# Reciprocal row sums applied after the weighted sum, and split keys and queries passed through DRAM, in the attention stage of a hybrid decoder kernel

## The chip, the cores and the metric

The kernel runs on one core of a Trainium2 chip. The metric is device time in microseconds (us) of one execution. The core has five engines that run their own instruction queues in order: TensorE (PE in the profile, with its weight loads listed apart as PEld), VectorE (DVE), ScalarE (ACT), GpSimd (POOL) and SyncE (SP), whose queue issues all DMAs of this kernel. PSUM is the memory that TensorE writes; SBUF is the on-chip memory that all engines read and write; DRAM tensors are reached by DMA only.

## What is computed

The reference is a two-layer decoder trunk over 1040 tokens (16 learned meta tokens and 1024 real ones) of width 1024. Layer 0 is a gated linear recurrence with a convolutional feed-forward block, layer 1 is the attention that the change is about, again with a feed-forward block. The attention (16 heads of width 64, a decay `c` per head and token, softmax over earlier tokens):

```
q = (x @ w_q).reshape(Bsz, T, B_HEADS, B_HDIM).transpose(0, 2, 1, 3)
...
for s, e in bounds:
    logits = jnp.einsum("bhqd,bhkd->bhqk", q[:, :, s:e], k[:, :, :e]).astype(jnp.float32) * scale
    logits = logits + (c[:, :, s:e, None] - c[:, :, None, :e])
    mask = jnp.arange(s, e)[:, None] >= jnp.arange(e)[None, :]
    p = jax.nn.softmax(jnp.where(mask, logits, -1e30), axis=-1)
    outs.append(jnp.einsum("bhqk,bhkd->bhqd", p.astype(v.dtype), v[:, :, :e]))
o = jnp.concatenate(outs, axis=2).transpose(0, 2, 1, 3).reshape(Bsz, T, D_MODEL)
return o @ w_out
```

## The kernel before, in words

Features lie on the 128 partitions and tokens along the free dimension. Each fp32 operand of a large matrix product is split into a high and a low part (`split`, lines 96 to 98: ACT casts a copy, DVE subtracts it from the source), and a product is three matmuls: high by high, high by low, low by high (lines 145, 148, 149). A matmul of 342 columns is the common size.

The attention stage weaves two streams into one hand-made order on TensorE (`weave`, in a manual schedule; the other engines' queues are ordered by the framework's scheduler). The first stream, `scores_ahead`, goes through 48 steps: 16 heads by three query blocks of 342 tokens (`BLK_B`), step s being head s // 3 and block s % 3. In step s it emits the weighted sums of step s (`sum_steps`) interleaved with the scores of step s + 1 (`score_steps`). The second stream, `dense`, projects values, keys and queries of the next pair of heads (`project`, in the order v0 v1 v2 k0 q0 k1 q1 k2 q2, the digit being the block), and at the end begins the output projection (`one`).

What one step does. `score_steps` takes three tiles of 114 queries. Per tile, TensorE multiplies the split queries by the split keys into PSUM (lines 879, 880) and adds the causal mask (line 882); DVE adds the decays and takes the row minimum (line 884, tile `L`); ACT takes the exponential with the row sum as a by-product (line 887, into `c4`); DVE takes the reciprocal of the sum (line 888) and multiplies the row tile by it (line 889). `sum_steps` turns the probabilities by TensorE transposes (line 909, PSUM tile `g`), ACT copies the high part out (line 913, `pTh`), DVE subtracts the low part (line 914, `pTl`), and two matmuls per key tile accumulate the output in the one `po` buffer of PSUM (lines 921, 922). The transposes run two key tiles ahead of the sums (`AHEAD`). At the end of a step ACT copies one half of `po` and DVE adds the other half (lines 933, 934), and SP writes 64 rows to the DRAM tensor `o_dram` (line 936).

Keys and queries. `project` leaves the scaled product of a pair of heads in one tile each (`k` in unit 17, `q` in unit 18; lines 798, 800). `halves(n, i)` then builds, for head n and block i, the operands of the score matmuls: `ks` with the high part of the keys on one half of the partitions and the low part on the other half (ACT line 837, DVE line 838), and two query tiles `qs` (high over low, and low over high; ACT lines 841, 842, 844, DVE line 843). That is four ACT and two DVE instructions of 64 partitions for each of 48 calls. Because the pair's tiles are reused, the dense stream waits before it writes k or q until the preceding pair's second head has been split. `halves` also loads the decays, broadcast from `c_dram` to 128 partitions (line 835). The first pair is projected earlier, by `heads0`, between the blocks of the preceding normalisation (`post`).

SP's queue in this stage holds the output writes of line 936, the decay loads of line 835 and the weight loads of line 115. GpSimd multiplies each loaded weight tile by the norm gain (line 126). Temporary tiles come from small rings: `u`, `y`, `sq` and `acc` have two buffers, `sq2` and `rstd` one (`SMB`).

Of the kernel before, what the change touches and what calls it, by code (L numbers as in the profile page):

```python
# [55 lines left out]
def tile_yoco(ctx: ExitStack, tc: tile.TileContext, hT, gains, lbl, w_in, head_g, w_oa,  # L56
# [228 lines left out]
    c_dram = nc.dram_tensor("csum", [BH, T], F32, kind="Internal").ap()  # L285

# [474 lines left out]

    KS, QS, VS, CN = [24, 25], [(33, 34), (6, 7)], [[35, 36], [4, 5]], [12, 13]
# [21 lines left out]
    def project(which, hp, i):  # L784

        p = pair[hp]
        if which not in p:
            src, c0, g, u = {"k": (kv_w, 0, 8, 17), "v": (kv_w, D, 8, 16), "q": (w_q, 0, 4, 18)}[which]
            p[which] = (WA.cols(src, [c0 + hp * P], gsb[:, g]), unit(u, which))
# [4 lines left out]
        while hp and which != "v" and ("split", 2 * hp - 1, i) not in seen:  # L794
            yield None
        with tc.high_priority(offset=OFF):
            if which == "q":
                V.scalar_tensor_tensor(dst[:, sl], pt, -HD ** -0.5, r2[:, sl], ALU.mult, ALU.mult)
            else:
                V.tensor_mul(dst[:, sl], pt, r2[:, sl])  # L800
# [25 lines left out]
    def halves(n, i):  # L826
# [6 lines left out]
        a, b = (hi, lo) if n % 2 else (lo, hi)  # L833
        sl = slice(BLK_A[i][0], BLK_A[i][0] + BLK_A[i][1])
        nc.sync.dma_start(h["c"][:, sl], c_dram[n:n + 1, sl].to_broadcast([P, BLK_A[i][1]]))
        x, k = pair[n // 2]["k"][1], h["k"]
        A.copy(k[a, sl], x[a, sl])
        V.tensor_sub(k[b, sl], x[a, sl], f(k[a, sl]))
        sl = slice(BLK_B[i][0], BLK_B[i][0] + BLK_B[i][1])
        x, (q1, q2) = pair[n // 2]["q"][1], h["q"]  # L840
        A.copy(q1[a, sl], x[a, sl])
        A.copy(q2[b, sl], x[a, sl])
        V.tensor_sub(q2[a, sl], x[a, sl], f(q1[a, sl]))
        A.copy(q1[b, sl], f(q2[a, sl]))
# [19 lines left out]
    def score_steps(s):  # L864
# [4 lines left out]
        out = h[g] = []  # L869
        for i in range(3):  # L870
# [5 lines left out]
            for x, (a, b) in enumerate(pcs):  # L876
# [9 lines left out]
                if last:  # L886
                    A.activation(L[:QT, :kn], L[:QT, :kn], AF.Exp, scale=-1.0, bias=c4[:, x:x + 1], accum_out=c4[:, 5:6])
                    V.reciprocal(c4[:, 6:7], c4[:, 5:6])
                    V.tensor_scalar(L[:QT, :kn], L[:QT, :kn], c4[:, 6:7], None, ALU.mult)  # L889
# [3 lines left out]
    def sum_steps(s):  # L893
# [31 lines left out]
        for kt in range(nk + AHEAD):  # L925
            if kt < nk:
                yield turned(kt)
            if kt >= AHEAD:
                yield summed(kt - AHEAD)
        r, r_ = (hi, lo) if j else (lo, hi)  # L930
        hp, sl = n // 2, slice(g0, g0 + gn)
        ot = o_last[0][:, sl] if hp == KT - 1 else tmp("sq", gn)
        A.copy(ot[r], av[r, :gn])
        V.tensor_add(ot[r], ot[r], av[r_, :gn])
        if hp < KT - 1:
            nc.sync.dma_start(o_dram[hp][r, sl], ot[r])
# [139 lines left out]
```

## Time and profile before

| what | value |
|---|---|
| median of 3 runs | 2878.49 us (2877.14 to 2882.29) |
| the profiled execution | 2883.05 us, its span 2881.1 us |
| PE, PEld busy | 2768.6 us (96%), 2709.2 us (94%) |
| DVE busy | 1830.8 us (64%) |
| ACT busy | 1258.2 us (44%) |
| POOL busy | 369.6 us (13%) |
| DMA | 163.14 MB, mean 57 GB/s |

Busy times are of the whole span. The page's slices of DVE go from 5 tenths in the feed-forward blocks to 8 tenths in the attention, so that an average over the span says little about this stage; the stage lies between about 1455 and 2040 us. PEclk in a window is the granted TensorE clock as a share of its upper level. Idle time of the weight loads (PEld) shows a wait of TensorE more sharply than that of PE, since matmuls are pipelined and their modelled durations overlap.

### The profile page before, as it was taken

Reading aid. Unit: us, or ns where it says so; the run is one execution under the profiler, and the core shown is the slowest. Engines: PE = TensorE matmul, PEld = TensorE weight load, DVE = VectorE, ACT = ScalarE, POOL = GpSimd, SP = SyncE. Lnnn points to the kernel's source line nnn. Section 1 sums busy time; section 2 is a strip of 40 time slices with the busy share of each in tenths; the row PEclk is TensorE's granted clock in tenths of the full one; section 3 lists DMA queues with packets and bytes.
Section 4 is the critical chain, followed back from the end, with each engine's and each line's share of the span. In section 5 each row is a group of like instructions: output and inputs, shape, how many; then the busy total and the mean of one; then the engine's idle time right before and its main releaser. Section 6 shows DMA issues by size and latency. Waiting matters only on the chain. (4 is left out here: it accounts for less than half of the span.)

```text
span 2881.1 us, 45581 instructions
## 1 busy us (share of the span) xinstructions
PE 2768.6 (96%) x17706; PEld 2709.2 (94%) x17706; DVE 1830.8 (64%) x3737; ACT 1258.2 (44%) x2421; POOL 369.6 (13%) x741
## 2 busy tenths in 40 slices
PE   8999999989999999999889999999989999999997
PEld 8999999989999999999789988898989999999997
DVE  5545445285655655566878888887684665565566
ACT  6445445455322322233566666666555232232232
POOL 2000000041100000004400000000240100010012
PEclk9999999999999999999899999999999999999999
DMA  4111111142211111112311111112242111121103
GB/s 132 30 38 30 38 40 49 37 125 62 66 38 52 45 52 38 44 52 67 92 45 45 45 45 45 45 45 93 70 124 59 45 52 52 30 65 39 52 30 113
DMA packets 202921, 163.14 MB, mean 57 GB/s; under 512 B 13984, under 2 KB 194128, under 8 KB 202704
## 3 DMA queue, kind: packets, MB, share of 16 engines
q1 hardware_dynamic: 202704, 160.23, 19.2%
q8 instruction: 138, 2.26, 0.3%
q14 instruction: 79, 0.65, 0.1%
HBM read 139.53 MB, written 20.66 MB: 56 GB/s over the span
## 5 line engine op out<-in xcount | busy, mean ns | idle before, releaser
L145 PE MATMUL pj<-x,wh 128*128 128x342 f32 (+1 forms) x2640 | 871.1, 330 | 12.6 <-DVE u L607 6.3
L149 PE MATMUL pj<-x,wl 128*128 128x342 f32 (+1 forms) x2640 | 849.3, 322 | 2.8 <-DVE wl L98 2.8
L148 PE MATMUL pj<-x,wh 128*128 128x342 f32 (+1 forms) x2640 | 849.3, 322 | 0.0
L145 PEld LDWEIGHTS pj<-x,wh 128*128 128x128 f32 x2640 | 500.8, 190 | 18.9 <-DVE u L607 7.2
L149 PEld LDWEIGHTS pj<-x,wl 128*128 128x128 f32 x2640 | 499.9, 189 | 3.1 <-DVE wl L98 3.1
L148 PEld LDWEIGHTS pj<-x,wh 128*128 128x128 f32 x2640 | 501.5, 190 | 0.1
L145 PE MATMUL g<-h,wh 128*128 128x342 f32 (+1 forms) x1056 | 339.0, 323 | 0.3
L149 PE MATMUL g<-h,wl 128*128 128x342 f32 (+1 forms) x1056 | 337.7, 321 | 0.4 <-DVE wl L138 0.4
L148 PE MATMUL g<-h,wh 128*128 128x342 f32 (+1 forms) x1008 | 323.8, 322 | 0.0
L97 ACT CAST wh<-raw 128x1024 fp32r<-128x1024 f32 x142 | 146.0, 1045 | 341.6 <-PE g L148 282.1
L145 PE MATMUL pj<-hnh,wh 128*128 128x356 f32 (+1 forms) x720 | 261.8, 364 | 9.3 <-ACT wh L97 7.0
L681 DVE TENSOR_TENSOR acc<-acc,g 128x342 f32<-128x342 f32 (+1 forms) x288 | 147.2, 511 | 193.6 <-PE g L149 193.4
L98 DVE TENSOR_TENSOR wl<-raw,wh 128x1024 fp32r<-128x1024 f32 x142 | 180.6, 1281 | 87.1 <-ACT wh L97 76.3
L149 PE MATMUL pj<-hnh,wl 128*128 128x356 f32 (+1 forms) x720 | 233.1, 324 | 0.8 <-DVE wl L98 0.8
L148 PE MATMUL pj<-hnl,wh 128*128 128x356 f32 (+1 forms) x720 | 232.8, 323 | 0.0
L612 ACT ACTIVATE y<-u,cw 128x342 f32<-128x342 f32 (+1 forms) x258 | 150.5, 584 | 182.6 <-DVE u L607 171.9
L188 POOL TENSOR_TENSOR acc<-acc,sq 128x342 f32<-128x342 f32 (+1 forms) x162 | 168.9, 1049 | 426.5 <-ACT sq L187 396.4
L613 DVE SCALAR_TENSOR_TENSOR y<-u,cw,y 128x342 f32<-128x342 f32 (+1 forms) x258 | 148.5, 576 | 111.4 <-ACT y L612 111.2
L607 DVE TENSOR_TENSOR u<-pj,r 128x342 f32<-128x342 f32 (+1 forms) x258 | 132.2, 513 | 114.1 <-PE pj L149 110.8
L145 PEld LDWEIGHTS g<-h,wh 128*128 128x128 f32 x1056 | 198.7, 189 | 2.5 <-ACT h L97 0.6
L149 PEld LDWEIGHTS g<-h,wl 128*128 128x128 f32 x1056 | 199.4, 189 | 0.6 <-DVE wl L138 0.6
L148 PEld LDWEIGHTS g<-h,wh 128*128 128x128 f32 x1008 | 190.6, 189 | 0.7 <-DVE h L98 0.2
(237 smaller groups left out, 4937.8 us busy)
## 6 DMA issues: line engine op xcount, KB each, us to landing
raw<-in_w_up_dram SPq DMA_DIRECT2D x84, 512.0 KB, 4.0
raw<-in_w_dn_dram SPq DMA_DIRECT2D x42, 512.0 KB, 4.7
raw<-in_w_in_dram SPq DMA_DIRECT2D x32, 512.0 KB, 4.1
raw<-in_kv_w_dram SPq DMA_DIRECT2D x16, 512.0 KB, 4.1
res<-h SPq DMA_DIRECT2D x44, 171.0 KB, 2.8
h<-mix SPq DMA_DIRECT2D x40, 171.0 KB, 2.2
cn<-csum SPq DMA_DIRECT2D x32, 171.0 KB, 3.6
raw<-in_w_oa_dram SPq DMA_DIRECT2D x8, 512.0 KB, 3.5
```

The costliest lines, as they stand in the source:

```text
L97: A.copy(hi, src)
L98: V.tensor_sub(lo, src, f(hi))
L145: PE.matmul(pt, wh, xh[:, sl], start=(j == 0), stop=False)
L148: PE.matmul(pt, wh, xl[:, sl], start=False, stop=False)
L149: PE.matmul(pt, wl, xh[:, sl], start=False, stop=(j == n - 1))
L188: eng.tensor_add(acc, acc, sq)
L607: V.tensor_mul(u[:, 2:], pt, r()[:, sl])
L612: A.activation(y, u[:, 2:], AF.Copy, scale=cw[:, j, 2:3])
L613: V.scalar_tensor_tensor(y, u[:, 1:n + 1], cw[:, j, 1:2], y, ALU.mult, ALU.add)
L681: V.tensor_add(acc_u[ot][:, sl], acc_u[ot][:, sl], pt)
```

## The change

Three things are changed.

1. The row tile of exponentials is no longer multiplied by the reciprocal sum. The reciprocals of the three tiles of a step go into a small tile `rg` and from there by a DMA to a new DRAM tensor `r_dram` (one row per head). At the end of `sum_steps` a DMA broadcasts the step's 342 reciprocals to 64 partitions (tile `rr`, in the `rstd` ring), and the output is multiplied by it.
2. At the end of a step, ACT copies both halves of `po` to 64 partitions, and GpSimd adds them and multiplies by `rr`. For the last pair of heads ACT and DVE do it as before, with one more DVE multiply.
3. `project` splits keys and queries once for the pair on 128 partitions (ACT cast, DVE subtract) into temporary tiles and writes the two parts to a new DRAM tensor `kq_dram`. `halves` has no ACT or DVE instructions left: it loads `ks` by two and `qs` by four DMAs of 64 partitions. The wait of the dense stream for the preceding pair's split is gone.

```
-            src, c0, g, u = {"k": (kv_w, 0, 8, 17), "v": (kv_w, D, 8, 16), "q": (w_q, 0, 4, 18)}[which]
-            p[which] = (WA.cols(src, [c0 + hp * P], gsb[:, g]), unit(u, which))
+            src, c0, g = {"k": (kv_w, 0, 8), "v": (kv_w, D, 8), "q": (w_q, 0, 4)}[which]
+            p[which] = (WA.cols(src, [c0 + hp * P], gsb[:, g]), unit(16, "v") if which == "v" else kq_dram["kq".index(which), hp])
...
-        while hp and which != "v" and ("split", 2 * hp - 1, i) not in seen:
-            yield None
         with tc.high_priority(offset=OFF):
-            if which == "q":
-                V.scalar_tensor_tensor(dst[:, sl], pt, -HD ** -0.5, r2[:, sl], ALU.mult, ALU.mult)
+            if which == "v":
+                V.tensor_mul(dst[:, sl], pt, r2[:, sl])
             else:
-                V.tensor_mul(dst[:, sl], pt, r2[:, sl])
+                x, xh, xl = tmp("u", n), tmp("y", n, F32R), tmp("acc", n, F32R)
+                if which == "q":
+                    V.scalar_tensor_tensor(x, pt, -HD ** -0.5, r2[:, sl], ALU.mult, ALU.mult)
+                else:
+                    V.tensor_mul(x, pt, r2[:, sl])
+                split(xh, xl, x)
+                for j, part in enumerate((xh, xl)):
+                    nc.sync.dma_start(dst[j][:, sl], f(part))
...
-        a, b = (hi, lo) if n % 2 else (lo, hi)
+        r = (lo, hi)[n % 2]
...
+        for j, rows in enumerate((lo, hi)):
+            nc.sync.dma_start(f(h["k"][rows, sl]), kq_dram[0, n // 2, j][r, sl])
         nc.sync.dma_start(h["c"][:, sl], c_dram[n:n + 1, sl].to_broadcast([P, BLK_A[i][1]]))
-        x, k = pair[n // 2]["k"][1], h["k"]
-        A.copy(k[a, sl], x[a, sl])
-        V.tensor_sub(k[b, sl], x[a, sl], f(k[a, sl]))
...
-        A.copy(q1[a, sl], x[a, sl])
-        A.copy(q2[b, sl], x[a, sl])
-        V.tensor_sub(q2[a, sl], x[a, sl], f(q1[a, sl]))
-        A.copy(q1[b, sl], f(q2[a, sl]))
+        for x, q in enumerate(h["q"]):
+            for j, rows in enumerate((lo, hi)):
+                nc.sync.dma_start(f(q[rows, sl]), kq_dram[1, n // 2, j ^ x][r, sl])
...
-                    V.reciprocal(c4[:, 6:7], c4[:, 5:6])
-                    V.tensor_scalar(L[:QT, :kn], L[:QT, :kn], c4[:, 6:7], None, ALU.mult)
+                    V.reciprocal(rg[:, i:i + 1], c4[:, 5:6])
+                    if i == 2:
+                        nc.sync.dma_start(r_dram[n, g0:g0 + 3 * QT].rearrange("(i q) -> q i", q=QT), rg)
...
+        rr = tmp("rstd", gn)
+        if hp == KT - 1:
+            nc.sync.dma_start(rr[r], r_dram[n:n + 1, sl].to_broadcast([HD, gn]))
+            ot = o_last[0][:, sl]
+            A.copy(ot[r], av[r, :gn])
+            V.tensor_add(ot[r], ot[r], av[r_, :gn])
+            V.tensor_mul(ot[r], ot[r], rr[r])
+        else:
+            nc.sync.dma_start(rr[lo], r_dram[n:n + 1, sl].to_broadcast([HD, gn]))
+            ot, o2 = tmp("sq", gn)[lo], tmp("sq2", gn)[lo]
+            A.copy(ot, av[lo, :gn])
+            A.copy(o2, av[hi, :gn])
+            G.tensor_add(ot, ot, o2)
+            G.tensor_mul(ot, ot, rr[lo])
+            nc.sync.dma_start(o_dram[hp][r, sl], ot)
```

On TensorE the order of the attention stage stays as it was, instruction by instruction; a handful of small normalisation matmuls move by some places in the 100 us before it, where the first pair is projected. What changes are the queues of DVE, ACT, GpSimd and SP. Line numbers after the change are larger (914 becomes 922, 936 becomes 954, and so on).

DVE, around the end of step 3 (the scores of step 4 are being finished; `pTl` is the low part that the next sums wait for, `L` the row tiles). Before:

```order
L889 TENSOR_SCALAR L_13780<-L_13780,c_1815_13781 114x470
L889 TENSOR_SCALAR L_13790<-L_13790,c_1818_13791 114x584
L843 TENSOR_TENSOR qs_13865<-q_13740,qs_13864 64x342
L888 RECIPROCAL c_1824_13820<-c_1824_13820 114x1
L889 TENSOR_SCALAR L_13819<-L_13819,c_1824_13820 114x698
L934 TENSOR_TENSOR sq_13847<-sq_13847,po_13770 64x342
L914 TENSOR_TENSOR pTl_13244<-g_13875,pTh_13243 128x342
```

The same place after; `u`, `y` and `acc` are the projected queries of the next pair and their two parts:

```order
L895 RECIPROCAL rg_13836<-c_1846_13847 114x1
L98 TENSOR_TENSOR acc_13882<-u_13880,y_13881 128x342
L891 ISA L_13874,c_1852_13875<-pd_13894,cn_13456,c_1852_13875 114x350
L891 ISA c_1852_13875 114x1
L895 RECIPROCAL rg_13836<-c_1852_13875 114x1
L922 TENSOR_TENSOR pTl_13284<-g_13942,pTh_13283 128x342
```

The three multiplies, the query split of one head and the output add no longer stand ahead of the `pTl` subtract; the reciprocals stay, and one subtract on 128 partitions has come in.

SP, around the end of step 5, where the last query block of the second pair (heads 2 and 3) has just been projected (`ob` is the output write, `raw` a weight load, `cn` the decays). Before:

```order
L936 DMA ob<-sq_13847 64x342
L835 DMA cn_14287<-csum 128x356
L835 DMA cn_14287<-csum 128x342 x2
L936 DMA ob<-sq_14003 64x342
L115 DMA raw_14596<-in_w_q_dram 128x8x128
L936 DMA ob<-sq_14158 64x342
L115 DMA raw_15037<-in_kv_w_dram 128x8x128
```

After (the last four of these rows are followed by two more loads of the same two query tiles):

```order
L809 DMA kq<-y_14262 128x342
L115 DMA raw_15204<-in_kv_w_dram 128x8x128
L809 DMA kq<-acc_14263 128x342
L954 DMA ob<-sq_14251 64x342
L850 DMA qs_13931<-kq 64x342
L850 DMA qs_13932<-kq 64x342
L948 DMA rstd_14368<-rsum 64x342
```

The two writes of the split queries (`y` high, `acc` low) stand ahead of the output write of step 5, and the loads of the query tiles for step 8 stand behind it.

## Rows read from the trace of the kernel before

**Rows 1.** Busy us of each engine in windows: PE, PEld, DVE, ACT, POOL, then PEclk, DMA

```profile
1340.00:1455.00 115.00, 96.65 (x547) 91.22 (x545) 90.73 (x168) 62.43 (x131) 48.41 (x42) 0.88 0.31 91
1455.00:2040.00 585.00, 553.32 (x3682) 521.27 (x3683) 483.22 (x1352) 374.69 (x918) 34.16 (x18) 0.97 0.17 49
1740.00:1760.00 20.00, 17.40 (x104) 16.02 (x104) 15.69 (x42) 10.72 (x27) 3.79 (x2) 0.91 0.18 48
...
1960.00:1980.00 20.00, 14.03 (x61) 11.16 (x60) 16.29 (x31) 14.53 (x29) 0.00 (x0) 0.67 0.68 221
```

**Rows 2.** Waits of the weight loads, 1455 to 2040: us in total, times, longest

```profile
PEld po L922 <- DVE pTl L914: 19.3, 28, 2.4
PEld po L921 <- ACT pTh L913: 6.7, 14, 1.0
PEld g L909 <- DVE L L889: 6.4, 7, 1.8
PEld g L909 <- DVE pTl L914: 5.7, 11, 1.2
PEld pd L879 <- DVE c L884: 5.5, 6, 3.5
PEld pj L148 <- DVE ol L98: 4.7, 4, 3.1
```

**Rows 3.** VectorE by line, 1455 to 2040: busy us, mean ns, idle before

```profile
L889 DVE TENSOR_SCALAR L<-L,c 114x128 f32<-114x128 f32 (+2 forms) x144 | 88.6, 617 | 3.1
...
L838 DVE TENSOR_TENSOR ks<-k,ks 64x342 fp32r<-64x342 f32 (+1 forms) x42 | 25.0, 596 | 2.4 <-ACT ks L837 1.1
...
L843 DVE TENSOR_TENSOR qs<-q,qs 64x342 fp32r<-64x342 f32 x44 | 22.3, 506 | 3.5 <-ACT qs L841 2.8
L934 DVE TENSOR_TENSOR sq<-sq,po 64x342 f32<-64x342 f32 x42 | 21.4, 510 | 12.6 <-ACT sq L933 11.7
```

**Rows 4.** ScalarE by line, 1455 to 2040, same columns

```profile
L841 ACT CAST qs<-q 64x342 fp32r<-64x342 f32 x44 | 20.9, 475 | 12.2 <-DVE q L798 9.0 <-PE pd L879 2.9
...
L933 ACT COPY sq<-po 64x342 f32<-64x342 f32 x42 | 18.4, 437 | 7.8 <-PE po L922 7.3
```

**Rows 5.** GpSimd's commonest add, whole span, from the page's groups

```profile
L188 POOL TENSOR_TENSOR acc<-acc,sq 128x342 f32<-128x342 f32 (+1 forms) x162 | 168.9, 1049 | 426.5 <-ACT sq L187 396.4
```

**Rows 6.** Timeline near 1742: start, us, engine, instruction, idle before

```profile
1741.82 1.90 POOL L126 TENSOR_TENSOR raw<-raw,gsb 128x1024 f32<-128x1024 f32 x1 [36.31 <-DVE c L884]
...
1741.88 2.21 DVE L838 TENSOR_TENSOR ks<-k,ks 64x342 fp32r<-64x342 f32 x1
...
1745.46 0.65 PE L922 MATMUL po<-pTl,vs 114*128 114x342 f32 x1 [2.16 <-DVE pTl L914]
```

**Rows 7.** Waits of SP's queue, 1455 to 2040: us in total, times, longest

```profile
SPq L936 <- DVE sq L934: 229.7, 35, 13.7
```

**Rows 8.** Timeline of SP: three issues in a row, start and us together

```profile
1480.31 1.28 SPq L835 DMA_DIRECT2D cn<-csum  x3
```

**Rows 9.** DMA issues: count, KB each, median us from issue to landing

```profile
res<-h SPq DMA_DIRECT2D x44, 171.0 KB, 2.8
h<-mix SPq DMA_DIRECT2D x40, 171.0 KB, 2.2
...
ob<-sq SPq DMA_DIRECT2D x42, 85.5 KB, 2.0
```

**Rows 10.** Timeline of VectorE: last query block of pairs 1 and 6, and first use

```profile
1532.13 0.51 DVE L798 SCALAR_TENSOR_TENSOR q<-pj,r 128x342 f32<-128x342 f32 x1
...
1533.81 0.50 DVE L843 TENSOR_TENSOR qs<-q,qs 64x342 fp32r<-64x342 f32 x1
...
1543.38 0.58 DVE L884 CUSTOM_DVE_ANT_0 L<-pd,cn 114x406 f32<-114x406 f32 x1 [0.24 <-PE pd L880]
...
1893.20 0.50 DVE L798 SCALAR_TENSOR_TENSOR q<-pj,r 128x342 f32<-128x342 f32 x1
...
1909.31 0.57 DVE L884 CUSTOM_DVE_ANT_0 L<-pd,cn 114x406 f32<-114x406 f32 x1
```

More of the change, by code (lines that the diff above doesn't have):

```diff
@@ L285, in tile_yoco @@
     c_dram = nc.dram_tensor("csum", [BH, T], F32, kind="Internal").ap()
+    r_dram = nc.dram_tensor("rsum", [BH, T], F32, kind="Internal").ap()
+    kq_dram = nc.dram_tensor("kq", [2, KT, 2, P, T], F32, kind="Internal").ap()
     hn = [(unit(kt, f"hnh{kt}", F32R), unit(8 + kt, f"hnl{kt}", F32R)) for kt in range(KT)]
@@ L832, in halves @@
             h["c"] = unit(CN[n % 2], "cn")
-        a, b = (hi, lo) if n % 2 else (lo, hi)
+        r = (lo, hi)[n % 2]
         sl = slice(BLK_A[i][0], BLK_A[i][0] + BLK_A[i][1])
+        for j, rows in enumerate((lo, hi)):
+            nc.sync.dma_start(f(h["k"][rows, sl]), kq_dram[0, n // 2, j][r, sl])
         nc.sync.dma_start(h["c"][:, sl], c_dram[n:n + 1, sl].to_broadcast([P, BLK_A[i][1]]))
-        x, k = pair[n // 2]["k"][1], h["k"]
-        A.copy(k[a, sl], x[a, sl])
-        V.tensor_sub(k[b, sl], x[a, sl], f(k[a, sl]))
         sl = slice(BLK_B[i][0], BLK_B[i][0] + BLK_B[i][1])
-        x, (q1, q2) = pair[n // 2]["q"][1], h["q"]
-        A.copy(q1[a, sl], x[a, sl])
-        A.copy(q2[b, sl], x[a, sl])
-        V.tensor_sub(q2[a, sl], x[a, sl], f(q1[a, sl]))
-        A.copy(q1[b, sl], f(q2[a, sl]))
+        for x, q in enumerate(h["q"]):
+            for j, rows in enumerate((lo, hi)):
+                nc.sync.dma_start(f(q[rows, sl]), kq_dram[1, n // 2, j ^ x][r, sl])
         seen.add(("split", n, i))
@@ L869, in score_steps @@
         out = h[g] = []
+        rg = sm.tile([P, 3], F32, tag="rg", name=nm("rg"), bufs=2)[:QT]
         for i in range(3):
@@ L929, in sum_steps @@
                 yield summed(kt - AHEAD)
+        hp, sl = n // 2, slice(g0, g0 + gn)
         r, r_ = (hi, lo) if j else (lo, hi)
[L931 to L936, printed above, removed]
+        rr = tmp("rstd", gn)
[13 more added lines that the diff above has]
+            nc.sync.dma_start(o_dram[hp][r, sl], ot)
     def scores_ahead():
```

## The prediction, made before the changed kernel was run

> **What bounds the kernel now.** I read the windows first. From 1455 to 2040 us, the attention stage, PE is busy 553 of 585 us and its weight loads 521, and DVE 483, that is 83%; ACT stands at 64% and GpSimd at 6% [rows 1]. So TensorE sets the time, and DVE is the engine it can wait for. The waits of the weight loads say that it does. They come to 48 us in the six rows: 25.0 us for the low part `pTl` (lines 922 and 909), 6.4 us for the normalising multiply of line 889, 5.5 us for the row minimum of line 884, 4.7 us for the split of the output projection's operands, and 6.7 us for ACT's high part `pTh` [rows 2]. The second loss is the clock. The window's mean PEclk is 0.97, so 585 x 0.03 = 17.6 us of TensorE at full speed are lost (14.6 to 20.5 by the rounding); 20 x 0.33 = 6.6 of these lie at 1960 to 1980, where the output projection begins, and 20 x 0.09 = 1.8 at 1740 to 1760 [rows 1]. The last can be followed: at 1741.82 GpSimd starts a weight multiply of 1.90 us, at 1741.88 DVE starts a key subtract that takes 2.21 us, and at 1745.46 a matmul has waited 2.16 us for `pTl` [rows 6]. The stage can give at most about 48 + 17.6 = 66 us.
>
> **The matmuls.** Their number and order in this stage stay. All that can change is how long they wait, and the clock.
>
> **VectorE.** Line 889 goes: 144 instructions, 88.6 us. Lines 838 and 843 go: 25.0 and 22.3 us. Line 934 goes for seven pairs: 21.4 us [rows 3]. In come 42 subtracts on 128 partitions, one for each key or query projection in the window (line 838 has two heads per projection, 42 for 21 keys; the queries are as many), at the 0.51 us of line 843, which has the same 342 columns: 21.3 us; and six multiplies for the last pair, 3 us. DVE: 483 - 157.3 + 24.3 = 350 us.
>
> **ScalarE.** Lines 841, 842 and 844 go, and line 837, four groups of about 20.9 us: 84 us. In come 42 casts at 0.475 us and 42 more copies of `po` at 0.437 us [rows 4]: 38 us. ACT: 375 - 45 = 330 us.
>
> **GpSimd.** 84 adds and multiplies at 1.05 us, the time of a 342-column add [rows 5], 88 us, make 122 of 585 us with the 34 of now [rows 1]. Nobody on TensorE's path waits for them at once: their result goes to DRAM, and ACT needs the `sq2` buffer only at the end of the next step, some 585/48 = 12 us later. If GpSimd came over 10 us late, ACT would stand still with the exponentials and `pTh` queued behind the copy.
>
> **SP.** A pair of heads adds 12 writes of split parts, 36 loads, 6 writes and 6 loads of reciprocals to 15 DMAs: 75 issues at 1.28/3 = 0.43 us [rows 8] are 32 us of the pair's 73. The queue keeps up on average. But it stands still at each output write, 229.7 us in all and once 13.7 us [rows 7], and now loads that TensorE needs are queued behind that.
>
> **The sum of the waits.** A queue's wait behind other work grows about as busy over idle share. For DVE that goes from 0.83/0.17 = 4.9 to, with 350 us in a stage of some 555, 0.63/0.37 = 1.7, to 35%. This is a chosen rule; the bounds are no change and all. By it the waits for `pTl` fall by 16 of 25.0 us (0 to 25). The wait of 6.4 us for line 889 becomes one for the exponential that precedes it; I take 3 us off (0 to 6.4). Of the 5.5 us at line 884, 3.5 are one wait at the stage's first score, which stays; 1 comes off the rest. Of 4.7 us at the output projection I take 2, DVE having no backlog of splits there; of the 6.7 us for ACT, whose share falls from 64% to 59%, 1. Together 23 us (0 to 43).
>
> Clock: the fall near 1745 came at DVE's wait, and one other window of 0.91 at 1880 to 1900 is like it: 2 x 1.8 = 3.6 us back. Of the 6.6 us at 1960 I take half, of the other 7.4 us, at the stage's start and in the rounding, 2. Together 9 us (0 to 17.6).
>
> **What the new path costs.** The tightest place is the last query block of a pair, used by the even head. For pair 1 DVE takes the projection out of PSUM at 1532.13 and the block's first score is at 1543.38 on DVE, its matmul some 0.6 us earlier: until 1542.7 [rows 10]. The low part can be ready where the first subtract of that block ends now, 1534.3. Then: issue and landing 2.2 (the row of 171 KB writes), five issues 2.2, landing 2.0 (85.5 KB) to 2.8 [rows 9]: 1540.7 to 1541.5. The output write of the same step, on which SP stops in between, follows its sums by two copies (0.9) and two GpSimd instructions (2.1); I take it that it is ready before the low part has landed. So pair 1 has 1 to 2 us of slack; pair 6 has 1909.31 - 1893.20 = 16.1 us against 11.25 [rows 10], so 5 more. Six even heads have this case. I set 2 us for it (0 to 65, see the third rival). The other loads have a step more.
>
> The start, 1340 to 1455, has DVE at 79% and PEclk 0.88 [rows 1]. Two heads' splits leave, one pair's comes in, and the writes and loads go into SP's queue between those of the normalisation. I set 0 (a gain of 5 to a loss of 15).
>
> Sum: 23 + 9 - 2 = 30 us. The profiled execution of 2883.05 us, its span and the 1.95 us around it, becomes 2853; it was 4.6 us above the median of 2878.49, so the median becomes **2848 us**.
>
> A rule of the Trainium skill speaks against the GpSimd part. First the row: DVE's 2.21 us beside GpSimd's 1.90, where a subtract of that shape takes 0.51 [rows 3, 6]. The Trainium skill, SBUF: State Buffer, section Who interferes with whom, says that a DVE instruction with two SBUF inputs and a GpSimd instruction that reads SBUF block each other for a whole instruction; the row agrees. By that rule GpSimd, over three times as busy, could at the worst delay each of the 42 new subtracts by a whole 1.05 us instruction: 44 us more on DVE, 0.71 busy, 2.4 in place of 1.7, and the waits for `pTl` would fall by 12.5 in place of 16: the sum would be 26.5.
>
> **The rivals.**
>
> First, nearly all waits go: 48 - 3.5 of rows 2 and 15 of the clock, 60 us: 2818. For it: DVE would be idle for over a third of the stage. Against it: the chain transpose, `pTh`, `pTl`, sum has a length of its own.
>
> Second, that length decides: DVE's load is not what ends the waits for `pTl`, since ACT's copy comes first and the look-ahead is two key tiles. Then only lines 889 and the two small clock falls count: 3 + 4 = 7 us, 2871. For it: ACT still stands near 60%. Against it: the largest wait, 2.16 us, lay behind a DVE instruction [rows 6].
>
> Third, and slower: the last query block comes late because SP stands at an output write that waits for two ACT copies, the broadcast reciprocals and two GpSimd instructions. Price: six heads. If SP's stop holds the loads so long that they come 8 us after the need, TensorE loses 6 x 8 = 48 us, and each stop, far longer than the one at 1745, brings a fall of the clock of at least the 1.8 us of that window, 11 us: 2848 + 59 = 2907. It decides from 30/6 = 5 us per head, clock included, that is from some 3 us of lateness. For it: a stop of 13.7 us exists [rows 7]. Against it: stops end when a step's sums end, which is before the last projection's own chain is done.
>
> The Trainium skill, DMA: Bandwidth & Descriptors, section Rules for kernel authors, says that two transfers to disjoint halves of the partitions take turns on the same engines and one of 128 partitions is better. In rows, 85.5 KB lands in 2.0 us and 171 KB in 2.2 [rows 9]. By that rule, with four loads of 2.0 us in turn, the block is 8.0 - 4.2 = 3.8 us later, pair 1 by 2 to 3 us too late, and the sum 30 - 10 = 20, which lies in the forecast's own range.
>
> Fourth, the start: each of the three normalisation blocks waits once for a read and a write more, 2.8 + 2.2 us [rows 9], since the splits use the `u` and `y` buffers that it reads its residuals into: 15 us, 2863.
>
> **How the numbers follow.** Forecast (2834 to 2866) 0.56, first rival 0.10, second 0.11, third 0.15, fourth 0.08. The range, 2820 to 2882, leaves out half of the first and most of the third. About 0.2%, 6 us, is what a measurement of this kernel can tell from no change. Faster: 0.56 + 0.10 + 0.06 + 0.06 = 0.78; same: 0.05 of the second and 0.02 of the fourth, 0.07; slower: 0.15.
>
> **What would show it.** DVE near 350 us and 63% in the stage, ACT near 330, GpSimd near 120; waits for `pTl` below 12 us; no window of 0.91 in mid-stage. It is wrong if weight loads wait for DMA into the query tiles at every sixth step, if PE waits for ACT's `pTh` as long as now for DVE, or if the stretch before the first score grows by over 5 us.

## The result, and the profile after

The changed kernel takes 3031.76 us (median of 4 runs, 3024.79 to 3034.66) against 2878.37 of the kernel before in the same comparison: ratio 1.0527, 95% interval 1.0506 to 1.0548, or 153 us slower. The forecast was 2848 us, in a range of 2820 to 2882, with a chance of 0.78 for faster. Direction and range were both wrong.

Where the time went can be read off the scores of each pair's last query block. The first score of this block for the even head of pair 1 starts at 1542.7 us before and at 1565.4 after; the same for pair 6 at 1908.6 and 2021.6. Before, pairs 1 and 6:

```profile
1542.73 0.42 PE L879 MATMUL pd<-ks,qs 128*114 128x406 f32 x1
...
1908.63 0.35 PE L879 MATMUL pd<-ks,qs 128*114 128x406 f32 x1
```

After, pair 6 (pair 1 is shown below):

```profile
2021.59 0.65 PE L886 MATMUL pd<-ks,qs 128*114 128x406 f32 x1 [14.72 <-DMA qs<-kq]
```

So 23 us are lost by pair 1, 18 us more with each of the next five pairs (73.2 us per pair before, 91.2 after), and the last 40 us between there and the last step (two waits of 16.7 and 24.0 us, below). The stage's start has hardly moved: its first score is at 1452.1 before and at 1453.8 after.

The windows of the changed kernel, with the columns of [rows 1]: busy us of PE, PEld, DVE, ACT, POOL, then the granted clock, the share of the DMA engines' time and GB/s.

```profile
1340.00:1455.00 115.00, 97.07 (x545) 92.61 (x543) 84.77 (x168) 56.41 (x119) 46.71 (x41) 0.87 0.44 128
1455.00:2195.00 740.00, 577.54 (x3700) 544.27 (x3701) 367.95 (x1126) 332.46 (x828) 115.13 (x104) 0.88 0.49 96
...
1740.00:1760.00 20.00, 5.86 (x26) 5.14 (x27) 3.03 (x8) 1.36 (x5) 3.65 (x3) 0.66 0.57 126
...
2100.00:2120.00 20.00, 0.94 (x6) 0.59 (x4) 1.74 (x2) 2.37 (x4) 1.79 (x2) 0.50 0.66 111
```

The stage is 155 us longer (740 for 585) with the same matmuls, and DVE is busy for 368 us of it in place of 483 [rows 1]: the relief came, and no engine is the bound. Of the 155 us, PE is idle for 131 (162.5 in place of 31.7) and busy for 24 more: the same matmuls take longer, with a mean granted clock of 0.88 where it was 0.97. In the window of 1740, where PE had 17.4 us of work before [rows 1], it has 5.9, and no engine beside it has over 4. From 2100 to 2120 all of them nearly stand still while the DMA engines are at 0.66. Two things are to be seen there: the wait is for transfers, and the DMA engines are busy for 0.49 of the stage at 96 GB/s, where before they needed 0.17 for 49 GB/s [rows 1].

What TensorE waits for, 1455 to 2195 us (us in total, times, longest):

```profile
PE pd L886 <- DMA qs<-kq: 106.0, 12, 15.8
PE pj L145 <- ACT oh L97: 24.0, 1, 24.0
PE po L929 <- ACT pTh L921: 17.0, 2, 16.7
PE pd L887 <- DMA qs<-kq: 7.2, 9, 2.4
PE po L930 <- DVE pTl L922: 4.5, 6, 1.0
```

The first and the fourth row are the query tiles. Six of the waits, 11.1 to 15.8 us long, stand at the last query block of the even heads of pairs 1 to 6; five of 2 to 6 us at the block before. The second and third row name ScalarE, but it is not the cause. Its timeline shows that each stands behind a cast whose operand had not come (start, us, instruction, idle before):

```profile
2093.35 1.04 ACT L135 CAST wh<-raw 128x1024 fp32r<-128x1024 f32 x1 [17.23 <-DMA raw<-in_w_ob_dram]
...
2123.83 1.05 ACT L97 CAST oh<-of 128x1026 fp32r<-128x1026 f32 x1 [19.33 <-DMA of<-ob]
```

The first is a weight load of the output projection, the second its first load of the attention output. SP's queue issues both, and it is late. Its longest waits in the same window:

```profile
SPq L948 <- DMA rsum<-rg: 135.9, 27, 7.5
SPq L845 <- DMA kq<-y: 73.1, 17, 10.8
SPq L942 <- DMA rsum<-rg: 33.1, 5, 8.0
SPq L954 <- POOL sq L953: 28.9, 9, 5.2
SPq L850 <- DMA kq<-y: 28.2, 16, 6.1
```

Before, SP stood 230 us at the output write [rows 7]; now it stands 29 there (line 954) and 169 at the broadcast load of the reciprocals (lines 948 and 942), until their write has landed. It stands a further 101 at the loads of keys and queries (lines 845 and 850), until the writes of the high parts, `kq<-y`, have landed, and 35 until those of the low parts have.

One stop in full, pair 1. Its last low part is ready on DVE here:

```profile
1535.81 0.52 DVE L98 TENSOR_TENSOR acc<-u,y 128x342 fp32r<-128x342 f32 x1 [0.81 <-DMA kq<-acc]
```

SP's issues around it; a span of several us over `x3` or `x4` has a wait inside:

```profile
1531.00 6.94 SPq L850 DMA_DIRECT2D qs<-kq  x4
...
1544.28 0.37 SPq L897 DMA_DIRECT2D rsum<-rg  x1
...
1547.38 7.88 SPq L845 DMA_DIRECT2D ks<-kq  x3
...
1555.93 0.43 SPq L809 DMA_DIRECT2D kq<-y  x1
...
1556.94 0.74 SPq L809 DMA_DIRECT2D kq<-acc  x1
...
1560.74 1.09 SPq L850 DMA_DIRECT2D qs<-kq  x2
...
1562.99 2.37 SPq L850 DMA_DIRECT2D qs<-kq  x4
```

And the matmul that waits for these loads:

```profile
1565.41 0.68 PE L886 MATMUL pd<-ks,qs 128*114 128x406 f32 x1 [15.80 <-DMA qs<-kq]
```

The low part is ready at 1536.3 and its write is issued at 1556.9: 20.6 us in SP's queue. Of these, 7.9 went on three key loads, with one wait of 6.1 us for a write of split keys issued just before the reciprocals' write of 1544.28. The forecast had 6.4 to 7.2 us from the low part to the last load; until the matmul it took 29.1.

### The profile page after: what moved, and what is told of

It reads as the page before. It is cut to its first block, busy times and chain, and to the rows that moved or that the text cites. A ratio compares the mean times of both kernels' runs of the same rounds, so it can differ in the third digit from the quotient of the medians.

```text
span 3031.2 us, 46317 instructions
## 1 busy us (share of the span) xinstructions
PE 2788.7 (92%) x17706; PEld 2729.1 (90%) x17706; DVE 1710.1 (56%) x3509; ACT 1208.6 (40%) x2318; POOL 447.1 (15%) x825
```

## The experiments

Medians in us, each beside the kernel before on the same chip (2877.2 to 2878.6):

| kernel | us | ratio, 95% interval |
|---|---|---|
| changed kernel | 3031.8 | 1.0527 (1.0506 to 1.0548) |
| keys and queries only | 2896.2 | 1.0064 (1.0049 to 1.0079) |
| reciprocals only | 2870.6 | 0.9978 (0.9968 to 0.9988) |
| no small write | 2892.6 | 1.0054 (1.0037 to 1.0070) |
| small write not read | 2980.1 | 1.0354 (1.0339 to 1.0369) |
| runs of 12 bytes | 2907.1 | 1.0099 (1.0085 to 1.0113) |
| rows of 456 bytes | 2897.4 | 1.0066 (1.0052 to 1.0080) |
| three small writes | 3183.6 | 1.1055 (1.1041 to 1.1069) |
| a third of the small write | 3017.4 | 1.0471 (1.0451 to 1.0492) |
| small write spread out, not read | 2896.0 | 1.0059 (1.0042 to 1.0076) |
| 4 bytes, loads on GpSimd's queue | 3002.6 | 1.0426 (1.0410 to 1.0442) |
| keys and queries only, loads on GpSimd's queue | 2869.2 | 0.9965 (0.9952 to 0.9979) |
| 12 bytes, output DMAs on GpSimd's queue | 2909.6 | 1.0109 (1.0096 to 1.0122) |
| 12 bytes, loads on GpSimd's queue | 2897.4 | 1.0056 (1.0041 to 1.0071) |
| the same, output on DVE | 2877.7 | 1.0001 (0.9990 to 1.0012) |
| 456 bytes, loads on GpSimd's queue | 2881.6 | 1.0007 (0.9996 to 1.0018) |
| reciprocals only, runs of 12 bytes | 2866.8 | 0.9960 (0.9947 to 0.9974) |

The trace of the changed kernel left two theories. **W**: each step's write of the reciprocals, 342 packets of 4 bytes, holds the DMA engines, so that everything behind it lands late. **S**: SP's queue, which works in order, stands at the broadcast load until that write has landed, with the query loads behind it. The rival from the prediction, that the path of keys and queries is itself too long, is the third.

### Each half alone

Keys and queries through DRAM, with the normalisation and the output as before:

```
-                    V.reciprocal(rg[:, i:i + 1], c4[:, 5:6])
-                    if i == 2:
-                        nc.sync.dma_start(r_dram[...], rg)
+                    V.reciprocal(c4[:, 6:7], c4[:, 5:6])
+                    V.tensor_scalar(L[:QT, :kn], L[:QT, :kn], c4[:, 6:7], None, ALU.mult)
```

(and the last seven lines of `sum_steps` as before the change).

> Only the split keys and queries go through DRAM; the row tiles are normalised on VectorE and the output is added as in the kernel before. Theory W (the 342 writes of 4 bytes per step hold up the DMA engines, and all transfers behind them land late): without these writes no score matmul waits over 2 us for its queries, and the time is 2850 to 2885. Theory S (SyncE's queue stands at the broadcast load that waits for that write, with the query loads behind it): the same, 2850 to 2885. Theory N (the number of split writes and half loads is itself too much for SyncE's queue and the DMA engines): still above 2980.

It took 2896 us, 18 more than the kernel before, where both W and S had it no slower than 2885: it loses by itself, if little. TensorE's waits, same window:

```profile
PE pj L145 <- ACT oh L97: 13.4, 2, 13.2
PE pd L885 <- DMA qs<-kq: 11.4, 4, 5.2
```

The query tiles are late four times, and the output projection stands again: the loads of the attention output lie in SP's queue behind the last query loads.

The reciprocals and the output on GpSimd, with `project` and `halves` as before:

```
-                x, xh, xl = tmp("u", n), tmp("y", n, F32R), tmp("acc", n, F32R)
-                ...
+            if which == "q":
+                V.scalar_tensor_tensor(dst[:, sl], pt, -HD ** -0.5, r2[:, sl], ALU.mult, ALU.mult)
```

> Only the reciprocals go through DRAM and the output goes over GpSimd; keys and queries are split on ScalarE and VectorE as in the kernel before. Theories W and S: the small writes and the waits for them are still there, but nothing that TensorE needs soon is queued behind them; VectorE is relieved of 110 us, so 2850 to 2870. Theory N: the same. If instead GpSimd's late adds hold ScalarE at the output copies, 2890 to 2960.

At 2870.6 us it is a little faster than before, with the same small writes in it. SP stands at the same broadcast load for 116 us in 37 waits (1455 to 2040 us):

```profile
SPq L946 <- DMA rsum<-rg: 86.4, 32, 5.5
SPq L940 <- DMA rsum<-rg: 29.4, 5, 7.1
```

TensorE hardly waits for that: 4.6 us in all, at the output projection, whose weight loads come late there. Without the key and query traffic no load that TensorE needs soon stands behind the broadcast load. So the loss is the two halves together, 2896 + 2871 - 2878 = 2889 if they added, 3032 in fact.

### The small write: wait or hold

Without the write; the broadcast load reads another DRAM tensor, so that the normalisation is left out:

```
-                    if i == 2:
-                        nc.sync.dma_start(r_dram[n, g0:g0 + 3 * QT].rearrange("(i q) -> q i", q=QT), rg)
-            nc.sync.dma_start(rr[lo], r_dram[n:n + 1, sl].to_broadcast([HD, gn]))
+            nc.sync.dma_start(rr[lo], c_dram[n:n + 1, sl].to_broadcast([HD, gn]))
```

> The changed kernel without the write of the reciprocals; the broadcast load reads the decay sums instead, so that it waits for nothing (the normalisation is left out in effect). Theory W: 2835 to 2865, DMA packets of 1368 bytes near 70 ns in the mean as before. Theory S: the same time. Theory N: above 2990.

With the write, but still reading the other tensor, so that no load waits for it (the normalisation is left out here too):

> The changed kernel with the small writes kept, but the broadcast load reads the decay sums and so waits for no small write (the normalisation is left out in effect). Theory W: still 2950 to 3030, since query loads land late behind the small writes. Theory S: 2835 to 2875, since SyncE's queue no longer stands. Theory N: above 2990, and no difference to the run without the write.

2892.6 and 2980.1 us. The second lies in W's range and far from S's; the first is 28 us above what both gave it, so that something is lost beside the small write. Of the 139 us between the first and the changed kernel, 87 come with a write that nobody reads and 52 with the load that waits for it. SP's waits for the landing of the keys' high parts show the hold. First without the write, then with it, unread:

```profile
SPq L845 <- DMA kq<-y: 15.8, 17, 1.7
```

```profile
SPq L845 <- DMA kq<-y: 82.8, 18, 9.8
```

The same waits for the same writes of 171 KB are five times as long. In the trace's packet records of 1455 to 2040 us, the packets of 1368 bytes that carry keys and queries take 75 ns in the mean without the small write, 59 of them over 0.5 us; with it, unread, 105 ns, 756 over 0.5 us, the longest 4.4. The small packets themselves are listed with a median of 9 ns.

### What of the small write holds

Runs of 12 bytes, 114 in place of 342 of 4; the DRAM row is ordered query by query and the multiplies read the broadcast tile in that order:

```
-  nc.sync.dma_start(r_dram[n, g0:g0 + 3 * QT].rearrange("(i q) -> q i", q=QT), rg)
+  nc.sync.dma_start(r_dram[n, g0:g0 + 3 * QT].rearrange("(q i) -> q i", i=3), rg)
```

> The changed kernel with the reciprocals of a step written as 114 runs of 12 bytes in place of 342 of 4 bytes (the order in DRAM is query by query, and the two multiplies read the broadcast tile in that order); bytes, number of DMAs and the wait of the broadcast load stay. From the runs before: the small writes' hold on the DMA engines is 2980 - 2893 = 87 us, SP's wait for their landing 3032 - 2980 = 52 us. If both are paid per packet, a third of the first and between a third and all of the second stay: 2893 + 29 + 17 to 52 = 2939 to 2974 us, with stalls of some 4 to 10 us at the first score of the even heads' third block. If the cost hangs on the DMA or its bytes, or on the wait alone: 3020 to 3035 us as the changed kernel.

2907 us: 125 us back, more than if each packet had its price. SP's longest wait for the small write falls from 8.0 us to 2.6. Something of the hold is left: 445 of the packets of 1368 bytes take over 0.5 us, in the mean 89 ns.

Rows of 456 bytes; TensorE turns the tile of reciprocals and ScalarE copies it out at the start of `sum_steps`:

```
+            if kt == 0:
+                PE.transpose(pt[:3, gn:gn + QT], h_rg, ident[:QT, :QT])
+                rt = pu[0][0][:3, pu[0][1]:pu[0][1] + QT]
+                A.copy(rt, pt[:3, gn:gn + QT])
+                nc.sync.dma_start(r_dram[n, g0:g0 + gn].rearrange("(i q) -> i q", q=QT), rt)
```

> The changed kernel with the reciprocals of a step turned on TensorE (one transpose of 114 columns per step), copied by ScalarE and written as 3 rows of 456 bytes; the broadcast load waits for that write as before. 48 transposes at some 0.2 us are 9 us more on TensorE. If the cost is that of small packets, both the hold and most of SP's wait go: 2893 + 9 + 0 to 15 = 2902 to 2917 us. If it is SP standing at a load that depends on a fresh write, however that is cut, the 52 us stay: 2945 to 2960 us.

2897 us, 5 above the version without a write, with 48 transposes more; both forecasts were higher. The broadcast load still depends on a fresh write, and that costs no more than these 5 us once the write lands quickly. So S is no cause by itself: SP stands long because the hold is long.

Three writes of 114 packets of 4 bytes, each after its row tile:

```
-                    if i == 2:
-                        nc.sync.dma_start(r_dram[n, g0:g0 + 3 * QT].rearrange("(i q) -> q i", q=QT), rg)
+                    nc.sync.dma_start(r_dram[n, q0:q0 + QT].unsqueeze(1), rg[:, i:i + 1])
```

> The changed kernel with the reciprocals written by three DMAs of 114 packets of 4 bytes, each right after its row tile's reciprocal, in place of one DMA of 342: same packets and bytes, bursts of a third, two more issues of 0.43 us on SP per step (41 us in all). If what counts is how many small packets come in one burst, it comes near the runs of 12 bytes (114 packets at once, 2907 us): 2900 to 2935 us. If it is the number of small packets of a step, in one burst or three: 3000 to 3060 us.

3184 us, off both forecasts: the same packets in three bursts cost 152 us more. One of the three alone (two thirds of the outputs are not normalised):

```
+                    if i == 2:
+                        nc.sync.dma_start(r_dram[n, q0:q0 + QT].unsqueeze(1), rg[:, 2:3])
```

> The changed kernel with only the third row tile's reciprocals written, as 114 packets of 4 bytes in one DMA after the last reciprocal of the step; the other two thirds of each row of the DRAM tensor hold values put there once at the start, so two thirds of the outputs are not normalised. The broadcast load still waits for the write. Beside it stand 114 packets of 12 bytes in one DMA (2907 us), 342 of 4 bytes in one (3032) and three times 114 of 4 bytes (3184). If the cost is by the number of packets, whatever their size: 2900 to 2915 us. If each DMA of 4-byte packets costs what one of the three cost, (3184 - 2893) / 144 = 2.0 us of TensorE: 2893 + 48 x 2.0 = 2980 to 3000 us.

3017 us: a third of the packets costs nearly as much as all, above what either forecast gave it. Neither the number of packets nor the burst alone sets the price; 114 packets of 12 bytes cost 14.5 us and 114 of 4 bytes 125 over the version without a write. What the 12 bytes change besides the size is how many packets in a row fall into the same stretch of DRAM. By its access pattern the DMA of 342 goes query by query through three stretches 456 bytes apart, one of 114 through one: a third of the packets, but as many into each stretch. Three such DMAs in turn cost 291 us, over twice the 125 of one, as if stretches written side by side were paid once and stretches written in turn each time; two more issues per step are in that figure, and no run takes them out. One more run separates the places from the size: the write that nobody reads, each reciprocal 512 bytes from the next.

```
-    r_dram = nc.dram_tensor("rsum", [BH, T], F32, kind="Internal").ap()
+    r_dram = nc.dram_tensor("rsum", [BH, T, P], F32, kind="Internal").ap()
-  nc.sync.dma_start(r_dram[n, g0:g0 + 3 * QT].rearrange("(i q) -> q i", q=QT), rg)
+  nc.sync.dma_start(r_dram[n, g0:g0 + 3 * QT, 0].rearrange("(i q) -> q i", q=QT), rg)
```

> The version whose small write is made but not read (342 packets of 4 bytes, the broadcast load reads another DRAM tensor, so the normalisation is left out; it took 2980 us), with the DRAM tensor spread out: each reciprocal goes to a place of its own, 512 bytes from the next, in place of 4 bytes. Packets, their size and their number stay. If the hold comes of neighbouring packets writing into the same few hundred bytes of DRAM one after the other: it goes, 2893 to 2910 us, as without the write. If it comes of the 4-byte size itself: 2965 to 2995 us.

2896 us against 2980: the hold is gone, with the same 342 packets of 4 bytes. SP's wait for the keys' high parts is back at that of the version without a write:

```profile
SPq L845 <- DMA kq<-y: 17.5, 17, 2.3
```

The packets of 1368 bytes take 75 ns in the mean again, 67 of them over 0.5 us. So what holds is many small packets written next to each other in DRAM. Only distances of 4 and 512 bytes were tried; how far apart is enough, and what happens in the memory, these runs do not show.

The hold is on the transfers, not on SP's queue. The changed kernel with the loads of keys and queries on GpSimd's queue (`nc.sync` to `nc.gpsimd` in `halves`), the small write as it was:

> The changed kernel with the loads of the split keys and queries issued from GpSimd's queue; the 342-packet writes of the reciprocals and everything else stay on SP's queue. If the loss were SP's order alone (the query loads standing behind the broadcast load), moving them off SP would give back nearly all: 2865 to 2885 us. If the small packets hold the DMA engines whatever queue a transfer comes from, the price of the hold found before (87 us) stays on top of some 2865 us: 2930 to 2985 us, with 1368-byte packets of 2 to 4 us still in the trace.

3003 us, 29 better and above both forecasts, with this wait of TensorE left:

```profile
PE pd L886 <- DMA qs<-kq: 94.8, 10, 14.8
```

A load of a query tile there lands a median 6.8 us after its issue; with runs of 12 bytes on the same queue it is 4.1, with rows of 456 bytes 3.1. Whether the DMA engines or the memory behind them are held, the trace cannot tell: it does not list a packet's engine.

### The rest: which queue is late

With the hold gone the kernel is still 15 to 29 us slower than before. The half that loses, keys and queries alone, with its loads on GpSimd's queue:

```
-            nc.sync.dma_start(f(h["k"][rows, sl]), kq_dram[0, n // 2, j][r, sl])
+            nc.gpsimd.dma_start(f(h["k"][rows, sl]), kq_dram[0, n // 2, j][r, sl])
```

(and so for `q`).

> Only keys and queries through DRAM (normalisation and output as in the kernel before), with the loads of the split keys and queries issued from GpSimd's queue in place of SP's; the writes stay on SP's. That version with SP's queue took 2896 us, with 12 us of stalls at the even heads' third block, a stall of 13.6 us at the first matmul of the output projection and about 27 us at half clock behind it. If SP's order causes these (query loads behind output writes, the output projection's loads behind query loads), they go or nearly: 2860 to 2878 us, and the load of the attention output is issued near 1960 us as before the change. If the round trip itself is too long: 2890 to 2900 us, with the stalls where they were.

2869 us in place of 2896, as SP's order predicts. The wait of 13.2 us at the output projection is gone, and that for the query tile of pair 1 is down to 0.65 us:

```profile
1536.24 0.41 PE L885 MATMUL pd<-ks,qs 128*114 128x406 f32 x1 [0.65 <-DMA qs<-kq]
```

The write of that low part now leaves SP at 1527.84, 0.1 us after the subtract has ended:

```profile
1525.02 0.33 SPq L809 DMA_DIRECT2D kq<-y  x1
1527.84 0.53 SPq L809 DMA_DIRECT2D kq<-acc  x1
```

Is it the output's own DMAs that SP stands at? Runs of 12 bytes, with the broadcast load and the output write on GpSimd's queue instead:

> The changed kernel with runs of 12 bytes, and the broadcast load of the reciprocals and the output write issued from GpSimd's queue (next to the add and multiply that run there); the writes and loads of keys and queries stay on SP's queue. With all on SP's it took 2907 us. If SP's standing at these two is what makes the query loads and the output projection's loads late: 2860 to 2875 us. If SP's order of the rest (query loads that wait for the landing of their writes, weight loads behind them) is enough to make them late: 2890 to 2905 us, with the 17 us stall at the output projection still there.

2909.6 us, as 2907 with them on SP's queue and 5 above the second forecast, with a stall of 15.3 us at the output projection. So the loss does not hang on these two. Among the things that SP still stands at, 1455 to 2040 us, are these:

```profile
SPq L897 <- DVE rg L895: 63.1, 15, 19.4
SPq L845 <- DMA kq<-y: 37.8, 19, 3.3
SPq L850 <- DMA kq<-y: 22.7, 15, 3.1
```

The last two are loads that wait for their fresh writes, with the next writes behind them. The first is the small write itself, which stands until its reciprocals are there. Keys and queries alone lose without any small write (2896 us), so the first is not needed for a loss; how much each adds here, no run shows.

Both remedies together, runs of 12 bytes and the loads on GpSimd's queue:

> The changed kernel with both remedies: reciprocals in runs of 12 bytes, and the loads of keys and queries on GpSimd's queue. If the two halves add (reciprocals alone in runs of 12 bytes -11.5 us, keys and queries alone on GpSimd's queue -9.2 us against 2878.4): 2852 to 2862 us, faster than any so far. If GpSimd's queue now holds the loads behind its own multiplies, which wait for the broadcast reciprocals: 2866 to 2900 us, with waits of the first score of the even heads' third block for the query load again.

2897 us; they don't add. GpSimd works in order too, and it stands at the output add until ScalarE has copied (its waits, 1455 to 2040 us):

```profile
POOL sq L952 <- ACT sq L951: 93.8, 13, 14.5
```

The loads stand behind that add. GpSimd's queue also stands 114 us at the loads themselves until the split writes have landed, but where keys and queries alone were moved it stands there longer (160 us), and that version is faster than before the change. With the add and multiply on DVE, so that GpSimd has only loads and gain multiplies:

```
-            G.tensor_add(ot, ot, o2)
-            G.tensor_mul(ot, ot, rr[lo])
+        V.tensor_add(ot[r], ot[r], av[r_, :gn])
+        V.tensor_mul(...)
```

(One of ScalarE's two copies per step goes with it.)

> The changed kernel with runs of 12 bytes, the loads of keys and queries on GpSimd's queue, and the output's add and multiply on VectorE (as the changed kernel has them for the last pair), so that GpSimd's queue holds only the gain multiplies and the loads. With the two output instructions on GpSimd it took 2897 us, and there GpSimd stood 94 us at the add, waiting for ScalarE's copies. If that in-order queue is what held the query loads: 2852 to 2866 us. If the loads are late for the write's landing or for the small packets: 2885 to 2900 us.

2877.7 us: 20 of them back, which speaks for GpSimd's order as a cause, though the copy that went is in it too. It is 12 to 25 above the first forecast and below the second. TensorE still waits 10.3 us for query tiles. What else keeps the two halves from adding isn't settled. With rows of 456 bytes and the loads on GpSimd's queue:

> The changed kernel with the reciprocals written as 3 rows of 456 bytes (one more transpose on TensorE per step) and the loads of keys and queries on GpSimd's queue. Rows of 456 bytes on SP's queue took 2897 us. If SP's order made the remaining loss there (16 us at the output projection, 11 us at the even heads' third block): 2860 to 2872 us, above the version with runs of 12 bytes by the 9 us of the 48 transposes at most. If not: 2890 to 2900 us.

2881.6 us, 16 better than on SP's queue, and 10 above its forecast; query tiles come late at two steps, by 2.6 and 6.7 us.

Last, the reciprocals alone in runs of 12 bytes, the best of the study:

> Only the reciprocals and the GpSimd output of the change (keys and queries split on the engines as before), with the reciprocals written as 114 runs of 12 bytes. The same with runs of 4 bytes took 2870.6 us, without any stall of TensorE for SP's queue. If the small packets cost nothing where no load that TensorE needs stands behind them: 2868 to 2873 us. If they still cost something there (the 5 us gap where the output projection's weights begin): 2860 to 2867 us.

2866.8 us, 0.40% faster than the kernel before, at the upper end of the second expectation. The 3.8 us between it and the runs of 4 bytes are hardly clear of noise: the two intervals overlap a little.

## Why the prediction was wrong, step by step

**The engines' work** came out nearly as forecast. In the version with rows of 456 bytes on SP's queue, whose stage is nearly as long as before, DVE is busy for 360 us of 1455 to 2040 (forecast 350), ACT for 327 (330, and 48 small copies more), GpSimd for 117 (122). A new subtract was forecast at 0.51 us, from [rows 3]; it took 0.647 there:

```profile
L98 DVE TENSOR_TENSOR acc<-u,y 128x342 fp32r<-128x342 f32 (+1 forms) x42 | 27.2, 647 | 5.0 <-ACT y L97 4.4
```

That is 42 x 0.137 = 5.8 us more, and the trace shows where it comes from: 34 of the 42 took 0.50 to 0.53 us, and each of the eight longer ones (0.74 to 2.21 us) started while a GpSimd instruction was running. The longest delayed the next `pTl`, and TensorE waited for it:

```profile
1822.85 2.34 POOL L126 TENSOR_TENSOR raw<-raw,gsb 128x1024 f32<-128x1024 f32 x1 [8.94 <-DMA raw<-in_w_q_dram]
...
1823.36 2.21 DVE L98 TENSOR_TENSOR acc<-u,y 128x342 fp32r<-128x342 f32 x1
...
1825.93 0.41 PE L933 MATMUL po<-pTl,vs 114*128 114x228 f32 x1 [2.45 <-DVE pTl L925]
```

So the price of GpSimd beside DVE was paid in small part: 5.8 us of the 44 at the worst that the prediction worked out by the Trainium skill, SBUF: State Buffer, section Who interferes with whom. The eight rows agree with that rule.

**The waits that go** were over-sized. The version with reciprocals alone in runs of 12 bytes has these weight-load waits (1455 to 2040 us):

```profile
PEld po L928 <- DVE pTl L920: 16.5, 26, 1.6
PEld po L927 <- ACT pTh L919: 7.4, 13, 2.2
```

DVE is at 407 us there, and the first row stands at 16.5 where it was 19.3 [rows 2]. In the version with 456 bytes and loads on GpSimd's queue, DVE at 374, it is 11.5:

```profile
PEld po L933 <- DVE pTl L925: 11.5, 15, 2.7
```

The other row of `pTl`, at line 909 before, falls from 5.7 to 1.3 and 1.1. The rule of busy over idle share gave a fall of 16 of the 25.0 us of both; the runs show some 12 at best. The wait for `pTh` did not fall in either (6.7 before, 7.4 and 7.1). The clock falls in mid-stage did go in the version with reciprocals alone in runs of 12 bytes:

```profile
1740.00:1760.00 20.00, 18.98 (x130) 18.23 (x129) 13.38 (x44) 12.53 (x31) 5.70 (x5) 1.00 0.18 45
```

But the one at the output projection stayed (17.1 us at the lower of the two levels, 1.2 GHz, from 1952 on, where it was 13.7 from 1967 on). So the 32 us of waits and clock were, in the versions that lose nothing elsewhere, 9.2 for the one half and 11.5 for the other.

**The new path** is the step that failed. It was set at 2 us, with bounds of 0 to 65, and cost by estimate some 160 to 175: the 153 us by which the kernel is slower, and the 9 to 21 that the halves gain where nothing holds them. Three assumptions in it were wrong:

- The write of the reciprocals was counted as one issue of 0.43 us and nothing else. Its shape, 342 runs of 4 bytes next to each other, was never priced, though the diff shows it. It holds other transfers up: 87 us, and 52 more through the load that waits for it.
- The landings of 2.0 to 2.8 us were taken from [rows 9], where no such write is under way. SP's stop at a load that waits for a fresh write was not in the sum at all; the output write was the only place where SP was seen to stand [rows 7].
- The chain was costed for the case that SP issues each DMA when its operand is ready. Even without the small write the low part of pair 1 was ready at 1524.0, its write left SP at 1529.6, and the score came at 1536.7, after a wait for the query tile: 12.7 us for the 6.4 to 7.2 that the forecast had (lines of the version without the small write, below). And the loads were followed only to the query tiles; those of the output projection, behind them in the same queue, were not looked at. They cost 13 to 24 us in one wait.

```profile
1523.53 0.51 DVE L98 TENSOR_TENSOR acc<-u,y 128x342 fp32r<-128x342 f32 x1
...
1529.64 0.71 SPq L809 DMA_DIRECT2D kq<-acc  x1
...
1536.72 0.68 PE L886 MATMUL pd<-ks,qs 128*114 128x406 f32 x1 [5.74 <-DMA qs<-kq]
```

**The rivals.** The third named the right place, the last query block of the even heads, and the right sign. Its price of 8 us per head was too small (11.1 to 15.8), and its mechanism was wrong: SP stands 29 us at the output write now, less than before. That its 2907 us lies near the versions without the hold (2893 to 2907) is luck. The fourth, the start, fell: the first score came 1.7 us later, for the 15 of that rival. Of the tests named at the end, "weight loads wait for DMA into the query tiles at every sixth step" was the one that struck.

The rule on two transfers to disjoint halves (the Trainium skill, DMA: Bandwidth & Descriptors, section Rules for kernel authors) was not tried: no run here loads the tiles by single transfers.

## What to carry to other kernels

Before a column of a small tile is sent to DRAM, look at the runs that it makes there: many runs of a few bytes next to each other held up the other transfers here, and the listed duration of those packets, a median of 9 ns, does not show it. Three values per run, or a turn into rows on TensorE, took away 125 and 134 of the 139 us. Where a change puts transfers in an in-order queue, price the landing of what each one waits for, and follow the queue to the last load behind it, also that of the next stage; two changes that gain alone can lose together when they share it.

## What the hardware showed

- With writes of 342 packets of 4 bytes next to each other in DRAM, listed with a median of 9 ns, among its transfers, the stage has packets of 1368 bytes that take up to 5.2 us (median 59 ns, mean 114 in the changed kernel; without the write the mean is 75 and the longest 1.3 us, and with each reciprocal 512 bytes apart the mean is 75). 114 of them do nearly the same (mean 108, longest 6.3 us). A possible reason is that each such packet must wait for the one before it in the same stretch of memory; no trace here shows that. The Trainium skill, DMA: Bandwidth & Descriptors, section Specifications, says that below 512 bytes the engine reads, changes and writes back. The trace does not show that step, and size alone is not the price: packets of 4 bytes set apart, of 12 and of 456 bytes are all below 512 and hold far less or nothing.
- The hold reaches transfers of another queue: loads of query tiles from GpSimd's queue land after a median of 6.8 us with the small write, and of 3.4 where keys and queries alone were moved, without it. The Trainium skill, DMA: Bandwidth & Descriptors, section Issuing engines are not separate DMA queues, says that all queues share the 16 engines; the runs agree.
- On GpSimd's queue a load is listed with some 0.5 us of GpSimd's own time (four query loads 2.05 us), and the move off SP still gained 27 us.
- A subtract of 0.51 us on DVE took up to 2.21 us when it started beside a GpSimd instruction (eight of 42 in the version with rows of 456 bytes).
